# A decoder trunk on one core: five blocks of the stream turned by VectorE blocks and DMA instead of TensorE

## The chip, the cores and the metric

The kernel runs on 1 core of one Trainium2 chip. The time is the device time of one execution, in microseconds; lower is better. All times of before in this document come from one profiled execution or from the three timed runs beside it. "TensorE", "VectorE", "ScalarE", "GpSimd" and "SyncE" are the engines that the profile calls PE (its weight loads PEld), DVE, ACT, POOL and SP.

## What is computed

The reference is a two-layer decoder trunk on one sequence of 256 tokens with 2048 channels, in f32. Layer 0 mixes by causal pooling, layer 1 by latent attention with a shared key and value set; each layer ends in a SwiGLU FFN of width 5632. Cut to what matters:

```python
def modulate(h, shift, scale):
    return h * (1.0 + scale[:, None, :]) + shift[:, None, :]

h = modulate(rmsnorm(x, norm_mix[i]), shift_m, scale_m)
cq = rmsnorm(h @ w_dq, q_norm)              # queries, layer 1
q = (cq @ w_uq).reshape(B, S, H, Q_HEAD_DIM)
...
x = x + gate_m[:, None, :] * y
h = modulate(rmsnorm(x, norm_ffn[i]), shift_f, scale_f)
x = x + gate_f[:, None, :] * ((silu(h @ w_gate) * (h @ w_up)) @ w_down)
```

The shifts, scales and gates are themselves products of a 2048-vector with 2048 x 12288 weights per layer.

## The kernel before

The residual stream `x` lies in SBUF with tokens on the partitions: two token tiles of 128, each with 2048 channels, which the code treats as four blocks of 512 (`ND = 4`, `CH = 512`). A projection needs the stream the other way round, channels on the partitions. So each block is scaled by the norm (`scaled`, line 546, two pieces of 128 x 512), turned, and then modulated per channel (`modulated`, line 571).

Products are made to f32 accuracy from fp32r halves: every weight unit (512 x 512, 1 MB) is loaded by SyncE, ScalarE makes its upper half (`hl`, line 376), VectorE the rest as a lower half (line 378), and each block of the stream becomes an upper and a lower half in the same way (lines 583, 584). A unit is then 24 matmuls of 128 x 512 on line 422, in the order upper weight by upper block, upper weight by lower block, lower weight by upper block (`proj_unit`).

The turning has two forms. `turned_pieces` (line 558) uses TensorE: 8 transposes of 128 x 128 a block into PSUM (line 564). The FFN's inner activations of some chunks use the other form: VectorE turns 32 x 32 blocks in place (line 752), GpSimd's queue stores the tile to DRAM (line 754) and loads it back in another order (line 769); the weights that meet it have their rows permuted to fit.

Where the stream blocks are turned in layer 1:

- Queries: `hidden_q` makes the four blocks `hmx[0]` to `hmx[3]`. The first two are turned; the last two were kept, turned, from the shared keys and values. They are read by the four units of `w_dq`, which stand on TensorE behind the keys and values of the third group of heads (`keys_values(2)`, lines 1386 and 422) and ahead of those of the fourth. The query latent's norm (`Latent.norm`, lines 1336 to 1339) and its own 8 transposes (`Latent.turn`) follow.
- Last FFN: `start_ffn(1, ...)` begins six chunks at once. For each of its blocks it runs 12 units; block 0 has a path of its own (`first`), blocks 1 to 3 are scaled by `ahead(j + 1)` a few units before they are turned and modulated by `hidden(j + 1, pieces)`.

Beside all this runs a background: the modulation sums of later stages (line 213), one 1 MB weight tile each, a load on SyncE and one pass on VectorE; `plan` and `tick` say how many go with each unit.

A tile framework gives out buffers and semaphores and sets the order of each engine's instructions by its own estimates; the engines then run their lists in order. The buffers that matter here are the seven of the tag `t2k` (2 KB a partition: scaled pieces, turned tiles, reloaded tiles, whole modulated columns), six `raw` (loaded weights), six `hl` (halves of weights) and eight banks of PSUM (`ps`).

Of the kernel before, what the change touches and what calls it, by code (L numbers as in the profile page):

```python
# [17 lines left out]
P = 128  # L18
# [77 lines left out]
def tile_trunk(ctx: ExitStack, tc: tile.TileContext, a: dict, out: bass.AP):  # L96
# [22 lines left out]
    def t2k(shape, dt=F32):  # L119
        return work.tile(shape, dt, tag="t2k", bufs=7, name=nm("t2k"))  # L120
# [437 lines left out]
    def turned_pieces(pieces):  # L558
# [7 lines left out]
            pts.append(pt)  # L566
        return pts

    mod_ins, hid_ins = [None], [None]

    def modulated(pts, j, c_scale, c_shift, direct=False):
        flush()
# [165 lines left out]
    def ffn(l, hT, gate_name, begun, then):  # L738
# [7 lines left out]
            return proj(ffn_weights(l)[which][:, c], hT)  # L746

        def turn_blocks(c):
            turned[c] = []
            for tok in range(NT):  # L750
                blocks = t2k([P, CH])
                dve.transpose(out=blocks, in_=nat[c][tok])  # L752
                rows = dram.tile([P, CH], F32, name=nm("turned"))
                pool.dma_start(rows, blocks)  # L754
                turned[c].append(rows)

        def turned_halves(m, tok, full):
            order = "p k (b j) -> p k b j"
# [5 lines left out]
        def transposed(c):  # L764
            m = act_t([P, 2, KL, T])
            if c in TURNED_BY_DMA[l]:
                for tok in range(NT):
                    full = t2k([P, CH])
                    pool.dma_start(full.rearrange("p (b e) -> p b e", e=P),
                                   turned[c][tok].rearrange("(b i) (g e) -> (i g) b e", i=BLOCK, e=P))  # L770
                    halves = lambda tok=tok, full=full: turned_halves(m, tok, full)
                    if c == GROUPS[-1][0]:
                        halves()
                    else:
                        pending.append((1, halves))
                mids[c] = m
                return
            for tok in range(NT):
                pt = ps_t()
                for f in range(KL):  # L780
                    pe.transpose(pt[:, f * P:(f + 1) * P], nat[c][tok][:, f * P:(f + 1) * P], ident)  # L781
                v = pt.rearrange("p (f t) -> p f t", f=KL)
                ts_ = slice(tok * P, (tok + 1) * P)
                act.activation(m[:, 0, :, ts_], v, AF.Copy)
                dve.tensor_tensor(out=m[:, 1, :, ts_], in0=v, in1=m[:, 0, :, ts_].bitcast(F32), op=ALU.subtract)
            mids[c] = m
# [143 lines left out]
    def start_ffn(l, first, ahead, hidden, late):  # L930
# [3 lines left out]
        with tc.issue_after(mod_ins[0].ins), tc.issue_after(hid_ins[0].ins) if hid_ins[0] else nullcontext():  # L934
            for j in range(ND - 1):
                if l == 0 and j == 1:
                    for tok in range(NT):
                        sync.dma_start(aside[0][:, tok], back[tok])
                todo = KD // 2 if j + 1 >= ND - late else 0
                for n, (c, which) in enumerate((c, w) for c in begun for w in (GATE, UP)):  # L940
                    if n == 2 * len(begun) - 1:
                        hT.append(hidden(j + 1, pieces))
                    if l == 0 or j > 0 or c > 0:
                        begun[c][which].block(j, hT[j])
                    if n == 2 * len(begun) - 5:
                        pieces = ahead(j + 1)
                    if todo and (n > 1 or j > 0 or l > 0):
                        pump(1)
                        todo -= 1
                pump(todo)  # L950
# [440 lines left out]
    with tc.issue_after(mod_ins[0].ins):  # L1391
        kv = [keys_values(0)]
    hmx = []
    pieces = scaled(rstd, 0)

    def hidden_q():
        nonlocal pieces
        pts = turned_pieces(pieces) if len(hmx) < 2 else kept[len(hmx) - 2]
        if len(hmx) < 1:
            pieces = scaled(rstd, len(hmx) + 1)  # L1400
        hmx.append(modulated(pts, len(hmx), C_AM1, C_SM1))

    def last_of_background():
        plan(n_all + MIX_DQ, 0)
# [253 lines left out]
    def first(pair):  # L1658
# [14 lines left out]
        with tc.manual_schedule(engines=ordered):  # L1673
# [28 lines left out]
            run(g1[0], g1[1], u1[0], u1[1], g1[2], u1[2])  # L1702
        return h.hT[0]

    hT, begun = start_ffn(1, first, lambda j: scaled(rstd, j),
                          lambda j, pieces: modulated(turned_pieces(pieces), j, C_AF1, C_SF1), LATE)
    plan(0, FFN1_UNITS)
    ffn(1, hT, "ffn1", begun, lambda: None)

# [5 lines left out]
    return w.reshape(k // CH, n // CH, P, KL * CH)  # L1715


def laid_out(i):

    def columns(v):  # L1720
        return np.asarray(v).reshape(-1, P).T

    o = {n: np.asarray(i[n]) for n in ("x", "c", "positions", "mod_w", "final_norm")}
    o["vectors"] = np.concatenate([columns(i[n]) for n in (
        "c", "norm_mix", "norm_ffn", "kv_in_norm", "kv_norm", "q_norm", "pool_scale", "mod_b", "kv_mod_b")], 1)
    o["mod_wt"] = o["mod_w"].transpose(0, 2, 1)
    o["kv_mod_wt"] = np.asarray(i["kv_mod_w"]).T
    block = o["mod_w"][0].reshape(KD // 2, 2, P, 6, D)[:, :, :, 3:5, :CH]
    o["mod_block"] = block.transpose(0, 2, 1, 3, 4).reshape(KD // 2, P, 4 * CH)

# [6 lines left out]
    for n in ("w_dkv", "w_uk", "w_uv"):  # L1737
        o[n] = units(np.asarray(i[n]))
    o["pool_w"] = np.asarray(i["pool_w"])[0].reshape(-1, KL, P, CH).transpose(0, 2, 1, 3).reshape(-1, P, KL * CH)
    for n in ("w_dq", "w_o"):  # L1740
        o[n] = units(np.asarray(i[n])[0])
    for n in ("ffn_gate", "ffn_up", "ffn_down"):
        o[n] = np.stack([units(w) for w in np.asarray(i[n])])
    for l, chunks in enumerate(TURNED_BY_DMA):
        w = np.asarray(i["ffn_down"])[l].reshape(NF, KL, KL, BLOCK, ND, CH)[list(chunks)]
        o["ffn_down"][l, list(chunks)] = w.transpose(0, 4, 3, 1, 2, 5).reshape(len(chunks), ND, P, KL * CH)
    return o


# [16 lines left out]
```

## Time and profile before

| | us |
|---|---|
| median of 3 runs | 1890.53 (1888.92 to 1891.82) |
| profiled execution | 1889.67 |
| its span, first to last instruction | 1887.9 |
| TensorE busy | 1836.0 |
| VectorE busy | 1431.6 |
| ScalarE busy | 836.2 |
| GpSimd busy | 56.1 |

The granted TensorE clock is 0.992 on the mean. A group's line in the profile gives the source line, the engine, the operation, output<-input, count, busy time and mean length in ns. The chain of waits gives start, length, engine and line of what the end of the run hung on. "DMA to landing" is the time from the issue of a transfer until its last byte is there. The stages: conditioning sums and pooling to 166 us, first FFN to some 880 us, keys and values and queries from there to 997 us, heads to 1085, output projection to 1145, last FFN to the end.

### The profile page before, as it was taken

What the parts mean: (1) busy time and instruction counts of PE and PEld (TensorE: products, weight loads), DVE (VectorE), ACT (ScalarE), POOL (GpSimd) and SP (SyncE); (2) the same over time, 40 slices, a digit from 0 to 9 for tenths busy, and PEclk for the clock granted to TensorE, in tenths of its full rate; (3) what the DMA queues carried; (4) which work ended last, traced back from release to release, by engine and by line L of the source; (5) the groups of instructions that cost most, each with busy time, mean ns of one, the idle gap of its engine ahead of it and who ended that gap; (6) DMA issues with size and microseconds to landing.
All of it is one profiled execution on the core that took longest, in us unless ns stands there. A gap on an engine that the chain in (4) does not pass through costs nothing.

```text
span 1887.9 us, 21743 instructions
## 1 busy us (share of the span) xinstructions
PE 1836.0 (97%) x8629; PEld 1489.2 (79%) x8629; DVE 1431.6 (76%) x1437; ACT 836.2 (44%) x914; POOL 56.1 (3%) x82
## 2 busy tenths in 40 slices
PE   6689999999999999999999999999999999999998
PEld 2356888888888888888889888888888888888886
DVE  1247799999889798897898886889778666645557
ACT  3125643453433334344776635634444433443343
POOL 0000000000000000000110000000011000000000
PEclk9889999999999999999999999999999999999999
DMA  9999998889999899995594485988788776766651
GB/s 399 415 420 411 387 365 335 322 311 367 406 350 420 346 407 390 392 420 205 200 376 166 168 342 199 386 328 333 264 312 318 293 268 237 267 253 235 223 200 45
DMA packets 84280, 589.14 MB, mean 312 GB/s; under 512 B 9761, under 2 KB 10193, under 8 KB 15441
## 3 DMA queue, kind: packets, MB, share of 16 engines
q1 hardware_dynamic: 79346, 570.68, 77.8%
q0 software_dynamic: 4592, 16.78, 2.4%
q8 instruction: 68, 1.11, 0.2%
q10 hardware_dynamic: 240, 0.29, 0.0%
q14 instruction: 34, 0.28, 0.0%
HBM read 574.58 MB, written 13.13 MB: 311 GB/s over the span
## 4 chain that ended last, share of the span: by engine, by line
PE 93%; DMA 5%; DVE 0%; ACT 0%; SPq 0%; issue 0%; POOLq 0%; DVEq 0%; ACTq 0%
PE ps L422 80%; DMA raw<-in_mod_w_dram 5%; PE ps L431 2%; PE ps L1033 2%; PE ps L1386 1%; PE ps L258 1%; PE ps L1472 1%; PE ps L1578 1%; PE ps L1289 1%; PE ps L781 0%; PE ps L564 0%; PE ps L1475 0%; DMA raw<-in_mod_block_dram 0%; PE ps L1487 0%; PE ps L1527 0%; PE ps L1488 0%
## 5 line engine op out<-in xcount | busy, mean ns | idle before, releaser
L422 PE MATMUL ps<-hl,act 128*128 128x512 f32 x6672 | 1518.5, 389 | 0.0
L422 PEld LDWEIGHTS ps<-hl,act 128*128 128x128 f32 x6672 | 1250.3, 188 | 260.2 <-ACT act L1108 0.9
L376 ACT ACTIVATE hl<-raw 128x2048 fp32r<-128x2048 f32 x285 | 545.8, 1918 | 638.2 <-PE ps L422 413.0
L378 DVE TENSOR_TENSOR hl<-raw,hl 128x2048 fp32r<-128x2048 f32 x285 | 651.3, 2287 | 196.6 <-ACT hl L376 196.5
L213 DVE SCALAR_TENSOR_TENSOR raw<-raw,s_row 128x2048 f32<-128x2048 f32 x168 | 383.1, 2284 | 15.5 <-DMA raw<-in_mod_wt_dram 15.4
L258 PE MATMUL ps<-raw,s_strip 128*32 128x512 f32 x392 | 59.0, 688 | 38.3 <-DMA raw<-in_mod_w_dram 37.9
L722 DVE TENSOR_TENSOR act<-ps,act 128x512 f32<-128x512 f32 x96 | 63.9, 682 | 15.4 <-PE ps L422 15.4
L258 PEld LDWEIGHTS ps<-raw,s_strip 128*32 128x32 f32 x392 | 8.8, 116 | 68.7 <-DMA raw<-in_mod_w_dram 47.6
L431 PE MATMUL ps<-hl,act 128*128 128x512 f32 x192 | 47.6, 400 | 0.6 <-DVE act L527 0.5
L431 PEld LDWEIGHTS ps<-hl,act 128*128 128x128 f32 x192 | 35.1, 188 | 10.3 <-ACT act L514 2.5
L794 DVE TENSOR_TENSOR x<-ps,x 128x512 f32<-128x512 f32 x32 | 21.6, 688 | 20.0 <-PE ps L422 20.0
L544 DVE TENSOR_TENSOR hl<-raw,hl 128x2048 fp32r<-128x2048 f32 (+3 forms) x17 | 31.9, 1879 | 4.8 <-ACT hl L541 4.7
L265 DVE COPY t2k<-ps 128x256 f32<-128x256 f32 x4 | 1.7, 425 | 44.3 <-ACT t2k L264 44.3
L1033 PEld LDWEIGHTS ps<-act,act 128*128 128x128 f32 x128 | 25.0, 202 | 11.7 <-issue 8.4
L754 POOL DMA_DIRECT2D turned<-t2k x26 | 14.5, 556 | 649.6 <-DVE t2k L752 649.3
L451 ACT ACTIVATE junk<-x 128x512 bf16<-128x512 f32 x23 | 14.5, 629 | 42.1 <-DVE x L636 25.0
L856 ACT ACTIVATE t2k<-ps 128x512 f32<-128x512 f32 x24 | 14.2, 592 | 41.8 <-PE ps L422 41.8
L1033 PE MATMUL ps<-act,act 128*128 128x256 f32 x128 | 32.4, 406 | 0.0
L720 ACT ACTIVATE act<-ps 128x512 f32<-128x512 f32 x32 | 19.1, 596 | 29.2 <-PE ps L422 29.2
L860 DVE TENSOR_TENSOR t2k<-ps,t2k 128x512 f32<-128x512 f32 x24 | 16.5, 687 | 19.9 <-PE ps L422 19.9
L541 ACT ACTIVATE hl<-raw 128x2048 fp32r<-128x2048 f32 (+1 forms) x15 | 26.5, 1766 | 3.5 <-PE ps L422 3.5
L998 DVE COPY hl<-ps 128x256 f32<-128x256 f32 x4 | 1.7, 423 | 30.4 <-PE ps L997 30.4
(235 smaller groups left out, 1044.3 us busy)
## 6 DMA issues: line engine op xcount, KB each, us to landing
raw<-in_mod_wt_dram SPq DMA_DIRECT2D x136, 1024.0 KB, 6.8
raw<-in_ffn_up_dram SPq DMA_DIRECT2D x88, 1024.0 KB, 6.5
raw<-in_ffn_down_dram SPq DMA_DIRECT2D x88, 1024.0 KB, 6.8
raw<-in_ffn_gate_dram SPq DMA_DIRECT2D x87, 1024.0 KB, 6.5
raw<-in_mod_w_dram SPq DMA_DIRECT2D x48, 1024.0 KB, 13.8
raw<-in_kv_mod_wt_dram SPq DMA_DIRECT2D x32, 1024.0 KB, 9.6
raw<-in_w_o_dram SPq DMA_DIRECT2D x16, 1024.0 KB, 5.4
raw<-in_mod_block_dram SPq DMA_DIRECT2D x8, 1024.0 KB, 12.5
```

The lines of the kernel that those rows point to most:

```text
L213: dve.scalar_tensor_tensor(out=r, in0=r, scalar=1.0, in1=s_row, op0=ALU.mult, op1=ALU.mult, accum_out=self.sums[:, self.n:self.n + 1])
L258: pe.matmul(self.bank[m * STRIP:(m + 1) * STRIP, :], lhsT=weights(k), rhs=r[:, k, i, :], start=first, stop=last)
L376: hi_ins = act.activation(hi, r, AF.Copy)
L378: lo_ins = dve.tensor_tensor(out=lo, in0=r, in1=hi.bitcast(F32), op=ALU.subtract)
L422: pe.matmul(banks[tok], lhsT=t_[:, i, k, tok * P:(tok + 1) * P], rhs=w[:, k, :], start=first and n < len(part), stop=last and n >= len(ord ...
L431: pe.matmul(bank, lhsT=t_[:, i, k, tok * P:(tok + 1) * P], rhs=w[:, k, :], start=first and n == 0, stop=last and n == len(order) - 1)
L541: hid_ins[0] = act.activation(w[1], w[0], AF.Copy)
L544: dve.tensor_tensor(out=w[2][:, ks], in0=w[0][:, ks], in1=w[1][:, ks].bitcast(F32), op=ALU.subtract)
L720: act.activation(part, banks[tok], AF.Copy)
L722: dve.tensor_tensor(out=part, in0=banks[tok], in1=part, op=ALU.add)
L794: dve.tensor_tensor(out=sums, in0=bank, in1=sums, op=ALU.add)
L1033: pe.matmul(mixed[g][:, n % 2, :], lhsT=wp[g][:, k, ns], rhs=pool_all[g // 2][:, g % 2, k, :], start=k == 0, stop=k == KL - 1)
```

## The change

Five blocks, `hmx[0]` and `hmx[1]` of the queries and blocks 1 to 3 of the last FFN, take the second form of turning. `stored_blocks` turns both scaled pieces on VectorE and stores them; `loaded_blocks` loads a block back in two halves of 256 channels (`pairs`), two transfers each; `modulated_blocks` modulates from these tiles instead of PSUM. The weights and vectors that meet these blocks (`w_dq`, `ffn_gate` and `ffn_up` of layer 1, the norms, the layer's modulation) have their rows permuted ahead of time, which costs the chip nothing. The two query blocks are scaled, turned and stored before the second group of keys and values is written; the reload of the second is written behind the modulation of the first. In the last FFN `ahead` comes four units earlier. The scratch for the descriptors of GpSimd's transfers (`dynamic_dma_scratch_size`) goes from 1024 to 4096.

```diff
+    def stored_blocks(pieces):
+        stored = []
+        for piece in pieces:
+            blocks = t2k([P, CH])
+            dve.transpose(out=blocks, in_=piece)
+            rows = dram.tile([P, CH], F32, name=nm("turned"))
+            pool.dma_start(rows, blocks)
+            stored.append(rows)
+        return stored
+
+    def channels_first(rows):
+        return rows.rearrange("(b i) (g e) -> (i g) b e", i=BLOCK, e=P)
+
+    def turned_by_dma(pieces):
+        return loaded_blocks(stored_blocks(pieces))
+
+    def loaded_blocks(stored):
+        pairs = [t2k([P, NT * KL, 2 * BLOCK]) for _ in range(2)]
+        for tok in range(NT):
+            for h2 in range(2):
+                es = slice(2 * h2 * BLOCK, 2 * (h2 + 1) * BLOCK)
+                pool.dma_start(pairs[h2][:, tok * KL:(tok + 1) * KL, :], channels_first(stored[tok])[:, :, es])
+        return pairs
...
+    def modulated_blocks(pairs, j, c_scale, c_shift):
+        flush()
+        t_ = act_t([P, 2, KL, T])
+        for k in range(KL):
+            scale, bias = (cols[:, i, j * KL + k:j * KL + k + 1] for i in (c_scale, c_shift))
+            full, src = t2k([P, T]), pairs[k // 2][:, :, k % 2 * BLOCK:(k % 2 + 1) * BLOCK]
+            act.activation(full.rearrange("p (b j) -> p b j", j=BLOCK), src, AF.Identity, scale=scale, bias=bias)
+            act.activation(t_[:, 0, k, :], full, AF.Copy)
+            mod_ins[0] = dve.tensor_tensor(out=t_[:, 1, k, :], in0=full, in1=t_[:, 0, k, :].bitcast(F32), op=ALU.subtract)
+        return t_
...
-                    if n == 2 * len(begun) - 5:
+                    if n == 2 * len(begun) - (9 if l == DEPTH - 1 else 5):
                         pieces = ahead(j + 1)
...
-    pieces = scaled(rstd, 0)
+    stored = [stored_blocks(scaled(rstd, j)) for j in range(2)]
+    pairs = loaded_blocks(stored[0])
 
     def hidden_q():
-        nonlocal pieces
-        pts = turned_pieces(pieces) if len(hmx) < 2 else kept[len(hmx) - 2]
-        if len(hmx) < 1:
-            pieces = scaled(rstd, len(hmx) + 1)
-        hmx.append(modulated(pts, len(hmx), C_AM1, C_SM1))
+        nonlocal pairs
+        j = len(hmx)
+        hmx.append(modulated_blocks(pairs, j, C_AM1, C_SM1) if j < 2 else modulated(kept[j - 2], j, C_AM1, C_SM1))
+        if j == 0:
+            pairs = loaded_blocks(stored[1])
...
-    hT, begun = start_ffn(1, first, lambda j: scaled(rstd, j),
-                          lambda j, pieces: modulated(turned_pieces(pieces), j, C_AF1, C_SF1), LATE)
+    hT, begun = start_ffn(1, first, lambda j: turned_by_dma(scaled(rstd, j)),
+                          lambda j, pairs: modulated_blocks(pairs, j, C_AF1, C_SF1), LATE)
...
-    nc = bacc.Bacc("TRN2", target_bir_lowering=False, num_devices=1, dynamic_dma_scratch_size=1024)
+    nc = bacc.Bacc("TRN2", target_bir_lowering=False, num_devices=1, dynamic_dma_scratch_size=4096)
```

In the changed kernel the old lines 376, 378, 213 keep their numbers; 1387 (copy of keys) is 1415, 1378 (copy of values) is 1406, 582 and 583 are 601 and 602 for the five blocks and 617 and 618 for the kept ones, 1337 and 1339 are 1365 and 1367, 912 is 940.

TensorE's list loses the 40 transposes (4566 rows become 4526) and is otherwise the same, but for two matmuls that change place around the query latent's transposes. SyncE's list is the same.

GpSimd's queue in the queries' stage was empty; now these twelve transfers stand there between the two norms (`t2k_6346` and `t2k_6347` are the two halves of block 0, `t2k_6533` and `t2k_6534` those of block 1; `turned_6328` and `turned_6332` are the stores of block 0, `turned_6340` and `turned_6344` those of block 1):

```order
L575 DMA turned_6328<-t2k_6326 128x512
L575 DMA turned_6332<-t2k_6330 128x512
L590 DMA t2k_6346<-turned_6328 128x4x64
L575 DMA turned_6340<-t2k_6338 128x512
L575 DMA turned_6344<-t2k_6342 128x512
L590 DMA t2k_6347<-turned_6328 128x4x64
L590 DMA t2k_6346<-turned_6332 128x4x64
L590 DMA t2k_6347<-turned_6332 128x4x64
L590 DMA t2k_6533<-turned_6340 128x4x64
L590 DMA t2k_6534<-turned_6340 128x4x64
L590 DMA t2k_6533<-turned_6344 128x4x64
L590 DMA t2k_6534<-turned_6344 128x4x64
```

What moved: nothing, these are new. The buffers of the built program tie them further: `t2k_6347` lies where store 2 reads from, so its first load waits for that store to land; `t2k_6533` and `t2k_6534` lie where `t2k_6346` and `t2k_6347` lay, so block 1's loads wait until ScalarE has scaled from block 0's.

ScalarE in the queries' stage, before: from the weight split of the first unit of `w_dq` (`raw_6606`) over block 0 (`act_6504`) to the split of the third (`raw_6689`). The copies on lines 1387 and 1378 are keys and values of the third group.

```order
L376 ACTIVATE hl_6611<-raw_6606 128x2048
L1378 ACTIVATE act_6326<-ps_6389 128x512
L1387 ACTIVATE act_6425<-ps_6438 128x512
L376 ACTIVATE hl_6661<-raw_6656 128x2048
L582 ACTIVATE t2k_6505<-ps_6490,cols 128x256
L582 ACTIVATE t2k_6509<-ps_6490,cols 128x256
...
L583 ACTIVATE act_6504<-t2k_6517 128x256
L1387 ACTIVATE act_6425<-ps_6464 128x512
L1378 ACTIVATE act_6425<-ps_6521 128x512
L376 ACTIVATE hl_6694<-raw_6689 128x2048
```

The same place now (`act_6516` is block 0, `act_6573` block 1; `raw_6664` and `raw_6697` are the second and third unit of `w_dq`):

```order
L376 ACTIVATE hl_6619<-raw_6614 128x2048
L1406 ACTIVATE act_6352<-ps_6415 128x512
L601 ACTIVATE t2k_6517<-t2k_6346,cols 128x256
...
L602 ACTIVATE act_6516<-t2k_6529 128x256
L376 ACTIVATE hl_6669<-raw_6664 128x2048
L1415 ACTIVATE act_6451<-ps_6490 128x512
L1406 ACTIVATE act_6451<-ps_6539 128x512
L601 ACTIVATE t2k_6574<-t2k_6533,cols 128x256
...
L1406 ACTIVATE act_6451<-ps_6540 128x512
L376 ACTIVATE hl_6702<-raw_6697 128x2048
L602 ACTIVATE act_6573<-t2k_6582 128x256
```

What moved: block 0's rows now stand ahead of the second unit's split and the first copy of keys (`ps_6464`), and a copy and the third unit's split stand inside block 1, ahead of its last two upper halves.

VectorE around the query latent's norm, before (613 and on) and after:

```order
L378 TENSOR_TENSOR hl_6866<-raw_6856,hl_6865 128x2048
L1337 TENSOR_SCALAR sm_6757<-sm_6756 128x1
L213 SCALAR_TENSOR_TENSOR raw_6858,sums_5369<-raw_6858,s_row 128x2048
L1339 TENSOR_SCALAR t2k_6759<-ps_6587,sm_6758 128x512
L1337 TENSOR_SCALAR sm_6766<-sm_6765 128x1
L213 SCALAR_TENSOR_TENSOR raw_6861,sums_5369<-raw_6861,s_row 128x2048
L1339 TENSOR_SCALAR t2k_6768<-ps_6588,sm_6767 128x512
```

Now:

```order
L1365 TENSOR_SCALAR sm_6765<-sm_6764 128x1
L213 SCALAR_TENSOR_TENSOR raw_6784,sums_5369<-raw_6784,s_row 128x2048
L378 TENSOR_TENSOR hl_6874<-raw_6864,hl_6873 128x2048
L1367 TENSOR_SCALAR t2k_6767<-ps_6595,sm_6766 128x512
L1365 TENSOR_SCALAR sm_6774<-sm_6773 128x1
L213 SCALAR_TENSOR_TENSOR raw_6866,sums_5369<-raw_6866,s_row 128x2048
L1367 TENSOR_SCALAR t2k_6776<-ps_6596,sm_6775 128x512
```

What moved: the weight's lower half (line 378) went from ahead of the norm into it. Further up on VectorE, the two lower halves of block 1's last two pieces stand behind the `krT` row (line 940), a background sum and the third unit's lower half.

More of the change, by code (lines that the diff above doesn't have):

```diff
@@ L748, in turn_blocks @@
         def turn_blocks(c):
[L749 to L755, printed above, removed]
+            turned[c] = stored_blocks(nat[c])
         def turned_halves(m, tok, full):
@@ L768, in transposed @@
                     full = t2k([P, CH])
-                    pool.dma_start(full.rearrange("p (b e) -> p b e", e=P),
-                                   turned[c][tok].rearrange("(b i) (g e) -> (i g) b e", i=BLOCK, e=P))
+                    pool.dma_start(full.rearrange("p (b e) -> p b e", e=P), channels_first(turned[c][tok]))
                     halves = lambda tok=tok, full=full: turned_halves(m, tok, full)
@@ L1715, in units, with by_blocks @@
     return w.reshape(k // CH, n // CH, P, KL * CH)
+def by_blocks(v, blocks):
+    o, n = np.array(v), [CH * b + r for b in blocks for r in range(CH)]
+    w = o[n].reshape((len(blocks), KL, KL, BLOCK) + o.shape[1:])
+    o[n] = w.transpose((0, 2, 3, 1) + tuple(range(4, w.ndim))).reshape((-1,) + o.shape[1:])
+    return o
 def laid_out(i):
@@ L1721, in columns @@
         return np.asarray(v).reshape(-1, P).T
-    o = {n: np.asarray(i[n]) for n in ("x", "c", "positions", "mod_w", "final_norm")}
+    i = {n: np.asarray(v) for n, v in i.items()}
+    o = {n: i[n] for n in ("x", "c", "positions", "mod_w", "final_norm")}
+    early, late = range(2), range(1, ND)
+    turned = [g * ND + j for gs, js in (((0, 1), early), ((3, 4), late)) for g in gs for j in js]
+    last = [by_blocks(m, turned) for m in (i["mod_w"][1].T, i["mod_b"][1])]
+    i["norm_mix"] = np.stack([i["norm_mix"][0], by_blocks(i["norm_mix"][1], early)])
+    i["mod_b"] = np.stack([i["mod_b"][0], last[1]])
+    i["norm_ffn"] = np.stack([i["norm_ffn"][0], by_blocks(i["norm_ffn"][1], late)])
     o["vectors"] = np.concatenate([columns(i[n]) for n in (
         "c", "norm_mix", "norm_ffn", "kv_in_norm", "kv_norm", "q_norm", "pool_scale", "mod_b", "kv_mod_b")], 1)
-    o["mod_wt"] = o["mod_w"].transpose(0, 2, 1)
-    o["kv_mod_wt"] = np.asarray(i["kv_mod_w"]).T
+    o["mod_wt"] = np.stack([i["mod_w"][0].T, last[0]])
+    o["kv_mod_wt"] = i["kv_mod_w"].T
     block = o["mod_w"][0].reshape(KD // 2, 2, P, 6, D)[:, :, :, 3:5, :CH]
@@ L1739, in laid_out @@
     o["pool_w"] = np.asarray(i["pool_w"])[0].reshape(-1, KL, P, CH).transpose(0, 2, 1, 3).reshape(-1, P, KL * CH)
[L1740 to L1746, printed above, removed]
+    o["w_dq"] = units(by_blocks(i["w_dq"][0], early))
+    o["w_o"] = units(i["w_o"][0])
+    for n in ("ffn_gate", "ffn_up"):
+        o[n] = np.stack([units(i[n][0]), units(by_blocks(i[n][1], late))])
+    o["ffn_down"] = np.stack([units(by_blocks(w, chunks)) for w, chunks in zip(i["ffn_down"], TURNED_BY_DMA)])
     return o
```

## Prediction

> **What bounds the kernel now.** I read the page first, then the chain of waits, then the busy times in the two stages that the change touches. The page says that TensorE carries nearly the whole span:
>
> ```profile
> span 1887.9 us, 21743 instructions
> PE 1836.0 (97%) x8629; PEld 1489.2 (79%) x8629; DVE 1431.6 (76%) x1437; ACT 836.2 (44%) x914; POOL 56.1 (3%) x82
> PE 93%; DMA 5%; DVE 0%; ACT 0%; SPq 0%; issue 0%; POOLq 0%; DVEq 0%; ACTq 0%
> ```
>
> The 5% of DMA lies in the first 160 us. After that, a microsecond of TensorE work that disappears is a microsecond of the span, and so is every microsecond for which TensorE has to wait for something new. The chain of waits, at the places where the blocks are turned (start, duration):
>
> ```profile
> 955.75 0.87 PE ps L564 x8
> 956.62 5.49 PE ps L422 x24
> 962.12 0.87 PE ps L564 x8
> 962.99 21.78 PE ps L422 x96
> 984.76 5.75 PE ps L1386 x48
> 991.43 0.66 PE ps L564 x6
> 992.09 4.80 PE ps L422 x21
> ...
> 1217.10 0.87 PE ps L564 x8
> 1217.97 65.30 PE ps L422 x288
> 1283.28 0.87 PE ps L564 x8
> ...
> 1349.45 0.87 PE ps L564 x8
> ```
>
> The first two groups of eight are the queries' blocks, the last three the FFN's. No gap stands around any of them. The 96 products from 962.99 are the four query blocks, 24 each at 0.227 us: 5.45 us a block.
>
> The other views that matter are the DMA share of some stretches, and how long the existing turned stores and reloads take to land. In the table, the last three columns are the granted clock, the DMA share and GB/s:
>
> ```profile
> 935.00:975.00 40.00, 40.00 (x231) 35.30 (x230) 39.93 (x41) 32.00 (x53) 0.00 (x0) 1.00 1.00 402
> 546.00:568.00 22.00, 22.00 (x99) 18.22 (x98) 21.96 (x18) 5.76 (x3) 2.65 (x4) 1.00 0.99 387
> 699.00:721.00 22.00, 22.00 (x99) 18.22 (x98) 20.84 (x16) 7.25 (x6) 2.65 (x4) 1.00 1.01 397
> 1638.00:1741.00 103.00, 103.00 (x456) 85.16 (x456) 55.36 (x38) 40.60 (x28) 8.48 (x13) 1.00 0.69 254
> ```
>
> In the queries' stage, 935 to 975, TensorE, VectorE (39.93 of 40) and DMA (1.00) are all full. In just such full stretches (546 to 721), the six turned stores and the six reloads landed after:
>
> ```profile
> L754 POOL DMA_DIRECT2D turned<-t2k x6: 542/558/569, 546.6 to 699.6; - x6
> DMA to landing us min/median/max: 5.4/6.8/8.0
> L769 POOL DMA_DIRECT2D t2k<-turned x6: 759/770/775, 552.6 to 713.5; - x6
> DMA to landing us min/median/max: 6.8/7.2/7.7
> ```
>
> Over the whole run the stores take 2.3/5.2/10.0 and the reloads 3.1/6.9/10.5 (least, median, most):
>
> ```profile
> DMA to landing us min/median/max: 2.3/5.2/10.0
> DMA to landing us min/median/max: 3.1/6.9/10.5
> ```
>
> **The change part by part.** *TensorE loses* 5 groups of 8 transposes: 5 x 0.87 = 4.35 us, all on the chain. That is 0.23% of the profiled execution's 1889.67 us, hardly more than the 0.2% that a measurement of this kernel can tell from no change.
>
> *The FFN's three blocks.* Each adds two VectorE transposes (row below), two stores and four reloads. Their scaled pieces exist at 1166.02, and the first block's columns are wanted after one more group of 24 products behind 1217.10, at 1222.5. With some 13 us of VectorE rows ahead of the transposes, 6.8 for a store, 3 for the issues and 7.2 for a reload, everything is there by about 1197. The cover is 25 us, and more than 40 for the other two blocks, so I cost this at nothing; gone, it would cost what it is late.
>
> ```profile
> L752 DVE STREAM_TRANSPOSE t2k<-t2k x26: 668/704/712, 545.6 to 1726.6; 128x512 f32<-128x512 f32 x26
> 1166.02 1.36 ACT L554 ACTIVATE t2k<-x,rstd 128x512 f32<-128x512 f32 x2
> ```
>
> *The queries' two blocks.* Here the cover is thin. These are the rows of before from which I walk the new order (the order itself is in the fences above):
>
> ```profile
> 937.11 2.29 DVE L378 TENSOR_TENSOR hl<-raw,hl 128x2048 fp32r<-128x2048 f32 x1
> 950.95 0.57 ACT L1378 ACTIVATE act<-ps 128x512 f32<-128x512 f32 x1
> 954.77 1.70 DVE L912 TENSOR_TENSOR krT<-t2k 32x256 f32<-32x256 f32 x4
> 957.12 1.00 ACT L582 ACTIVATE t2k<-ps,cols 128x256 f32<-128x256 f32 x2
> 958.02 0.72 ACT L583 ACTIVATE act<-t2k 128x256 fp32r<-128x256 f32 x2
> 960.15 0.60 ACT L1387 ACTIVATE act<-ps 128x512 f32<-128x512 f32 x1
> 961.24 1.92 ACT L376 ACTIVATE hl<-raw 128x2048 fp32r<-128x2048 f32 x1
> ```
>
> Let a store land S after its issue, a reload L after its issue. The first transpose follows the 937.11 row (its pitch is 2.2 us): store 1 is issued at 940.0. One L378 and one transpose later, at 942.9, comes store 2. Block 0's last three reloads wait for store 2 to land, because the second half's buffer is the one that store 2 reads, and are issued 0.77 apart. ScalarE's first row on block 0 needs the third of the four: 943.7 + S + L. With 6.8 and 7.2 that is 957.7. ScalarE has stood since 951.5, with a copy of keys and a weight split behind it; those have several us in hand. From there three scalings (0.5 each), a copy (0.5) and the first upper half (0.36) make 960.2. TensorE wants it at 962.99 - 1.74 = 961.25, so block 0 is just in time: nothing.
>
> Block 1 is not. Its reloads write the buffers of block 0, so the first waits for block 0's second scaling, the second for the fourth, at 957.7 + 3.6 = 961.3. The third of them, issued at 962.1, lands at 962.1 + 7.2 = 969.3. In general this is 948.1 + S + 2L. TensorE wants block 1's first upper half at 961.25 + 5.45 = 966.7, so ScalarE has to begin 1.36 earlier, at 965.3: it is 4.0 late. Then ScalarE's order puts a copy (0.6) and a weight split (1.9) between the third and fourth scaling and their upper halves: the third upper half comes 5.6 after ScalarE's begin, where TensorE wants it 1.36 + 0.91 after: 3.3 more. VectorE's order puts the krT row (1.70), a background sum (2.2) and a weight's lower half (2.2) ahead of the last two lower halves: 1.2 more. Sum 8.5. Bounds: with the fast ends (2.3 and 3.1) S + 2L is 8.5 and no term is left; with the slow ends (10.0 and 10.5) it is 31.0, the lateness 13.8 and the sum 18.3. I take the middle, since the rows of the full stretches are nearest: same queue, same DMA share.
>
> *The query norm behind it.* After the change VectorE does a weight's lower half (2.29) more between the first norm's small row (L1337) and the row that scales by it (L1339); the transposes of the query latent wait for these.
>
> ```profile
> 983.95 0.15 DVE L1337 TENSOR_SCALAR sm<-sm 128x1 f32<-128x1 f32 x1
> 984.01 2.29 DVE L213 SCALAR_TENSOR_TENSOR raw<-raw,s_row 128x2048 f32<-128x2048 f32 x1
> 986.74 0.75 DVE L1339 TENSOR_SCALAR t2k<-ps,sm 128x512 f32<-128x512 f32 x1 [0.43 <-POOL sm L1338]
> 990.19 0.75 DVE L1339 TENSOR_SCALAR t2k<-ps,sm 128x512 f32<-128x512 f32 x1 [0.43 <-POOL sm L1338]
> ```
>
> Before, the second L1339 ends at 990.94 and the last six transposes begin at 991.43. The extra row, less the 0.43 that VectorE waited anyway, is 1.9 us. Bounds: 0, if VectorE has caught up while TensorE stands, and 4.5, two rows.
>
> *The four times larger scratch.* Before, the second of two reloads is issued only when the first has landed:
>
> ```profile
> 706.11 0.76 POOL L769 DMA_DIRECT2D t2k<-turned  x1 [5.98 <-DMA turned<-t2k]
> 713.54 0.77 POOL L769 DMA_DIRECT2D t2k<-turned  x1 [6.67 <-issue]
> ```
>
> So the old scratch held one reload of 128 x 4 runs and not two; four times that holds the four reloads of a block, which have as many runs each, half as long. This I have used above. For the old FFN chunks it brings their reloads about 7 us forward. TensorE waits for none of them now, so this is worth nothing; below nothing neither, because nothing is queued behind them on GpSimd's queue but their like. SyncE's order of loads does not change. The added 2 MB in the queries' stage are 5 us at its 402 GB/s; they push the weights back, which had 6 to 10 us in hand. That is in the upper bound only.
>
> Sum: -4.35 + 8.5 + 1.9 = +6.05 on 1889.67, that is 1895.7 us. The median of the runs shown, 1890.53, stands 0.86 higher; I forecast on the profiled execution.
>
> **The rivals.** *A, the reloads are quick.* TensorE keeps its full 4.35: 1885.3 us, or 1887.2 if the norm's 1.9 stays. It decides at S + 2L below 12.7 (17.2, less 3.3 and 1.2). Stores landing after 2.3 and reloads after 3.1 speak for it, but those least values lie outside the full stretches; the full stretches themselves, at 19 and more, speak against it. [...]
>
> *B, the reloads land in time, but the order costs.* With S + 2L at 17.2 the lateness is gone, and 3.3 + 1.2 + 1.9 - 4.35 = +2.05 remain: 1891.7 us, no change that can be told. For it: ScalarE and VectorE stand for a while, so they free fewer weight buffers, SyncE issues fewer loads, and block 1's reloads may meet an emptier DMA than block 0's. Against it: VectorE goes on with four rows meanwhile.
>
> *C, the slow ends.* Reloads of 256-byte runs, with eight transfers queued behind each other, land as late as the latest rows: 18.3 + 1.9 - 4.35 = +15.9, 1905.5 us.
>
> **How the numbers follow.** The forecast gets 0.50, its own range 1893.5 to 1901. A gets 0.22, B 0.20, C 0.08. Faster by over 0.2% is A, 0.22; within it is B, 0.20; slower is the forecast and C, 0.58. The range goes down to 1885 to hold A, and up to 1903, leaving out most of C.
>
> **What would show it.** In the changed kernel the L564 rows fall from 72 to 32. Right would be: TensorE gaps behind the first 24 products of the queries' first block, in sum near 8 us and released by ScalarE (the upper halves) and VectorE (the lower halves); ScalarE's wait for the reload near 6 us from 951; no gap at 1217, 1283 and 1349. Wrong would be: the 96 products in one piece (A), or gaps of 4 to 5 us with the reloads of block 1 landing within 5 us (B), or TensorE waiting for weights in the FFN.

## The result, and the profile after

| | before | after |
|---|---|---|
| median of the runs beside each other | 1890.34 us (1888.92 to 1891.82) | 1901.58 us (1900.67 to 1902.55) |
| profiled span | 1887.9 | 1900.0 |
| granted TensorE clock, mean | 0.992 | 0.986 |
| L564 transposes on TensorE | 72 | 32 |

The changed kernel is slower: ratio 1.006, 95% interval 1.005 to 1.007. The forecast was 1895.7 us; the time lies in its range and on the side it gave the most chance, 5.9 us above the number and 0.6 us above the forecast's own range, 1893.5 to 1901. The loss of 11.2 us is nearly twice the 6.05 of the sum. The mean clock of one execution says little here: the fast runs of before span 0.986 to 0.993. In the page of the changed kernel, the span, the busy times and the chain by engine:

```profile
span 1900.0 us, 21734 instructions
PE 1839.8 (97%) x8589; PEld 1489.3 (78%) x8589; DVE 1437.5 (76%) x1447; ACT 837.3 (44%) x914; POOL 76.3 (4%) x112
PE 90%; DMA 6%; DVE 2%; issue 1%; ACT 1%; POOL 0%; SPq 0%; POOLq 0%; DVEq 0%; ACTq 0%
```

TensorE has 40 instructions fewer and is nevertheless 3.8 us longer busy (1836.0 before): the same products took longer somewhere. TensorE is 90% of the chain, 93% before. Its waits in the queries' stage and ahead of the heads, by what ended them (us in total, times, longest):

```profile
...
PE ps L422 <- ACT act L602: 7.1, 3, 5.0
...
PE ps L294 <- DVE cols L302: 2.0, 1, 2.0
```

Where they stand, in TensorE's timeline of the changed kernel (start, duration, count, idle time before and its releaser):

```profile
961.72 5.95 PE L422 MATMUL ps<-hl,act 128*128 128x512 f32 x24 [0.27 <-ACT act L602]
972.69 2.07 PE L422 MATMUL ps<-hl,act 128*128 128x512 f32 x4 [5.03 <-ACT act L602]
976.57 18.57 PE L422 MATMUL ps<-hl,act 128*128 128x512 f32 x68 [1.80 <-ACT act L602]
994.98 5.92 PE L1414 MATMUL ps<-act,hl 128*128 128x256 f32 x48
...
1002.63 0.88 PE L564 MATMUL ps<-con,t2k 128*128 128x128 f32 x6 [0.36 <-DVE t2k L1367]
...
1009.92 0.34 PE L294 MATMUL ps<-con,cols 128*16 128x128 f32 x1 [2.04 <-DVE cols L302]
```

Line 302 on VectorE ends the sums of a gate; TensorE turns their columns (`cols`) on line 294 before it goes on to the heads. The same products before, and what follows them:

```profile
962.75 22.02 PE L422 MATMUL ps<-hl,act 128*128 128x512 f32 x96
984.60 5.92 PE L1386 MATMUL ps<-act,hl 128*128 128x256 f32 x48
```

The 96 products of the queries' blocks now run from 961.72 to 994.98, 33.26 us from start to start against 21.85. Only 6.83 us of the difference are the waits of 5.03 and 1.80; the other 4.58 are in the products. Four of them took 2.07 us (972.69), 0.52 each against 0.227. The granted clock says why (busy times with counts, then clock, DMA share and GB/s):

```profile
967.50:972.60 5.10, 0.16 (x1) 0.00 (x0) 0.00 (x0) 1.36 (x4) 0.00 (x0) 0.99 0.93 312
972.60:976.50 3.90, 2.07 (x4) 1.16 (x4) 3.76 (x7) 3.90 (x8) 0.00 (x0) 0.50 0.04 15
976.50:980.00 3.50, 3.43 (x8) 2.51 (x9) 3.50 (x5) 3.50 (x11) 0.00 (x0) 0.50 0.47 112
982.00:985.00 3.00, 3.00 (x13) 2.40 (x12) 3.00 (x3) 3.00 (x8) 0.00 (x0) 0.89 0.75 309
1009.90:1012.60 2.70, 2.68 (x13) 2.70 (x14) 1.54 (x1) 0.27 (x1) 0.00 (x0) 0.52 0.78 246
```

After the wait of 5.03 us TensorE works at half clock (0.50) for about 10 us, and after the wait of 2.04 us ahead of the heads once more (0.52) for about 3.4. In the kernel before, the clock is 1.00 in both places.

The transfers behind the waits, on GpSimd's queue and on ScalarE:

```profile
940.59 0.63 POOL L575 DMA_DIRECT2D turned<-t2k  x1 [17.91 <-DVE t2k L573]
950.15 2.25 POOL L590 DMA_DIRECT2D t2k<-turned  x3 [0.46 <-issue]
960.56 0.75 POOL L590 DMA_DIRECT2D t2k<-turned  x1 [8.16 <-ACT t2k L601]
963.08 2.23 POOL L590 DMA_DIRECT2D t2k<-turned  x3 [1.77 <-ACT t2k L601]
```

```profile
959.00 1.09 ACT L601 ACTIVATE t2k<-t2k,cols 128x256 f32<-128x256 f32 x2 [6.22 <-DMA t2k<-turned]
971.24 1.09 ACT L601 ACTIVATE t2k<-t2k,cols 128x256 f32<-128x256 f32 x2 [5.25 <-DMA t2k<-turned]
974.31 1.90 ACT L376 ACTIVATE hl<-raw 128x2048 fp32r<-128x2048 f32 x1
```

Block 1's reloads are issued when ScalarE has scaled from block 0's (960.56, 963.08) and land for 971.24; the weight split that ScalarE does inside block 1 (974.31) stands ahead of the upper half that ends the second wait.

In the last FFN nothing waits. From the first full group of products on, TensorE's work is one piece to the end of the window shown (1400), where before it was cut by transposes at 1217, 1283 and 1349:

```profile
1182.65 217.54 PE L422 MATMUL ps<-hl,act 128*128 128x512 f32 x959
```

Against before, the trace runs 10.4 us late at the fourth group's keys (994.98), 11.4 at the query latent's last six transposes (1002.63), 14.7 at the end of the heads, and 12.1 at the end of the span: the FFN gives 2.6 us back.

### The profile page after: what moved, and what is told of

Same layout as the page of the kernel before. It is cut to its first block, busy times and chain, and to the rows that moved or that the text cites. A ratio compares the mean times of both kernels' runs of the same rounds, so it can differ in the third digit from the quotient of the medians.

```text
span 1900.0 us, 21734 instructions
## 1 busy us (share of the span) xinstructions
PE 1839.8 (97%) x8589; PEld 1489.3 (78%) x8589; DVE 1437.5 (76%) x1447; ACT 837.3 (44%) x914; POOL 76.3 (4%) x112
## 4 chain that ended last, share of the span: by engine, by line
PE 90%; DMA 6%; DVE 2%; issue 1%; ACT 1%; POOL 0%; SPq 0%; POOLq 0%; DVEq 0%; ACTq 0%
PE ps L422 77%; DMA raw<-in_mod_w_dram 4%; PE ps L431 2%; PE ps L1061 2%; PE ps L258 2%; DMA t2k<-turned 1%; PE ps L1501 1%; PE ps L1607 1%; DVE raw L213 1%; PE ps L1317 1%; DVE hl L378 0%; DMA raw<-in_ffn_gate_dram 0%; PE ps L809 0%; PE ps L1504 0%; DMA raw<-in_mod_block_dram 0%
## 5 line engine op out<-in xcount | busy, mean ns | idle before, releaser
L575 POOL DMA_DIRECT2D turned<-t2k x36 | 20.1, 558 | 661.5 <-DVE t2k L573 661.2
L573 DVE STREAM_TRANSPOSE t2k<-t2k 128x512 f32<-128x512 f32 x36 | 24.8, 701 | 3.5 <-DMA turned<-t2k 3.2
```

The source lines that it names most:

```text
L573: dve.transpose(out=blocks, in_=piece)
```

## Experiments

Ratios are to the kernel before, run beside each kernel on the same chip, with their 95% intervals. The intervals are some 2 us wide on each side, so terms of a microsecond are read from the traces.

**1 to 3: the parts one by one.** First the FFN's three blocks alone, with the queries' two back on TensorE:

```diff
-    early, late = range(2), range(1, ND)
+    early, late = (), range(1, ND)
...
-    stored = [stored_blocks(scaled(rstd, j)) for j in range(2)]
-    pairs = loaded_blocks(stored[0])
+    pieces = scaled(rstd, 0)
```

> Only the last FFN's three blocks are turned by VectorE and DMA; the queries' two are back on TensorE; the scratch is 4096. Theory (the whole loss lies in the queries' stage, the FFN's transfers are covered): 24 transposes of 0.109 us go and nothing waits, -2.6 us, about 1887.9 us against 1890.5, ratio 0.9986; TensorE's products of the last FFN in one piece from the first reload on. Rival (turning by DMA costs in itself, by its traffic or GpSimd's queue, about the same in every block): three fifths of the +11.2 us, 1897 us, ratio 1.0035, with gaps in the last FFN.

Measured: 1887.51 against 1890.7 us, ratio 0.9982 (0.9972 to 0.9991). Its last FFN is unbroken like that of the changed kernel. The theory holds: the three blocks bring what their transposes cost.

Then the queries' two alone:

```diff
-    early, late = range(2), range(1, ND)
+    early, late = range(2), ()
...
-                    if n == 2 * len(begun) - (9 if l == DEPTH - 1 else 5):
+                    if n == 2 * len(begun) - 5:
...
-    hT, begun = start_ffn(1, first, lambda j: turned_by_dma(scaled(rstd, j)),
-                          lambda j, pairs: modulated_blocks(pairs, j, C_AF1, C_SF1), LATE)
+    hT, begun = start_ffn(1, first, lambda j: scaled(rstd, j),
+                          lambda j, pieces: modulated(turned_pieces(pieces), j, C_AF1, C_SF1), LATE)
```

> Only the queries' two blocks are turned by VectorE and DMA; the last FFN's three are back on TensorE; the scratch is 4096. Theory (the loss lies in the queries' stage): the changed kernel's +11.2 without the FFN's -2.6, that is +13.8 us, about 1904.3 us, ratio 1.0073, with the same two gaps of 5 and 2 us on TensorE and a granted clock near 0.5 behind each. Rival (a like cost in every block): two fifths of +11.2, 1895 us, ratio 1.0024.

Measured: 1903.55 us, ratio 1.0068 (1.0055 to 1.008). TensorE's waits behind the first block are those of the changed kernel, 4.62 and 1.80 among the products and 2.04 ahead of the heads. But here the first block is late as well, by 1.95 us, where the changed kernel has 0.27:

```profile
963.75 5.92 PE L422 MATMUL ps<-hl,act 128*128 128x512 f32 x24 [1.95 <-ACT act L602]
974.29 2.08 PE L422 MATMUL ps<-hl,act 128*128 128x512 f32 x4 [4.62 <-ACT act L602]
```

The loss lies in the queries' stage, whole.

Then the scratch alone (`dynamic_dma_scratch_size=4096` in the kernel before):

> The kernel before with nothing changed but the scratch for descriptors, 4096 instead of 1024. Theory: the two reloads of an FFN chunk are now issued together, the second some 7 us earlier, and nobody waits for them: 0, ratio within 0.999 to 1.001. Rival (the earlier reloads are what shortens the last FFN, not the missing transposes): -2.6 us, ratio 0.9986; or, if they crowd out weights, above 1.002.

Measured: 1889.48 us, ratio 0.9992 (0.9983 to 1.0001), no difference that can be told from none. It does what was said of it: the second reload of a chunk is now issued 1.77 us after the first, where it was 7.43 (706.11 and 713.54 before). GpSimd's queue in this run:

```profile
705.95 0.76 POOL L769 DMA_DIRECT2D t2k<-turned  x1 [6.37 <-DMA turned<-t2k]
707.72 0.77 POOL L769 DMA_DIRECT2D t2k<-turned  x1 [1.01 <-DMA turned<-t2k]
```

**4: own buffers for the reloads.** If block 1 is late because its reloads wait for block 0's buffers, buffers of their own take that away:

```diff
...
-    pairs = loaded_blocks(stored[0])
+    both = act_t([P, 4, NT * KL, 2 * BLOCK], F32)
+    own.extend([both[:, 2 * j], both[:, 2 * j + 1]] for j in range(2))
+    pairs, pairs1 = (loaded_blocks(s) for s in stored)
```

> The changed kernel, but the reloads of the queries' two blocks go to a buffer of 8 KB of their own (a slot of the blocks' tag), so block 1's no longer wait for block 0 to be scaled; TensorE's and SyncE's lists are as in the changed kernel. Theory (the lateness is the chain of reload, scaling, reload through shared buffers): block 1's reloads are issued near 956 instead of 960.6 to 963.8 and are there near 966; the gap of 5.0 us behind the first 24 products falls below 1.5, the granted clock behind it stays over 0.9, and the 96 products take 24 to 26 us instead of 33.3: about 1893.5 us (1892 to 1897). The wait of 2 us ahead of the heads stays. Rival (the DMA is full, so eight reloads together land as late as two times four): the gap stays at 4 us or more and the time at 1900 or above.

Measured: 1901.37 us, ratio 1.0052 (1.0038 to 1.0066). The theory falls. The wait behind the first 24 products has gone, but block 0 now comes late. TensorE, ScalarE and GpSimd of this run:

```profile
967.08 20.52 PE L422 MATMUL ps<-hl,act 128*128 128x512 f32 x78 [6.74 <-ACT act L603]
```

```profile
961.89 1.09 ACT L602 ACTIVATE t2k<-act,cols 128x256 f32<-128x256 f32 x2 [13.11 <-DMA act<-turned]
962.89 1.89 ACT L376 ACTIVATE hl<-raw 128x2048 fp32r<-128x2048 f32 x1
```

```profile
957.72 1.49 POOL L590 DMA_DIRECT2D act<-turned  x2 [6.00 <-DMA turned<-t2k]
```

Block 0 was there 2.9 us later than in the changed kernel (961.89 against 959.00), although its last three reloads were issued earlier (949.47 against 950.15); why they took longer is not shown. A weight split of 1.9 us got between its scaling and its upper halves. Block 1's reloads still wait, for its stores: issued from 948.40 on, these land at 957.7, after 9 us. So in these two builds the buffers decide which block is late, not whether one is.

**5: no pause for TensorE.** Twenty products that nobody reads fill the wait:

```diff
         proj_unit(cq, hmx[j], hi, lo, j == 0, j == ND - 1)
+        if j == 0:
+            spare = ps_t()
+            for n in range(20):
+                k = n % KL
+                pe.matmul(spare, lhsT=hmx[0][:, 0, k, :P], rhs=hi[:, k, :], start=n == 0, stop=n == 19)
```

> The changed kernel with 20 spare products of 128x512 (into a bank that nobody reads) on TensorE between the first 24 products of the queries and the next, 4.5 us in the place of the 5.0 us wait; they are extra work, and the output is unchanged. In this build ScalarE's copy and weight split also move out of block 1, and the gate's cols row (L302) comes ahead of the head weights on VectorE. Theory (the wait halves the granted clock, and that costs 4.6 us in the products and 1.3 at the heads on top of the waits): the granted clock stays at 1.00 through the stage, the last 72 products take 16.4 us instead of 22.3 (waits counted), and the time is about 1892 us (1890 to 1895). Rival (the low clock in the records costs nothing, the products are late for their halves of weights): only the moved rows help, 1.8 and 2.0 us, 1897.5 us or more, with gaps among the 72 products.

Measured: 1904.28 us, ratio 1.0076 (1.0062 to 1.009). The theory is right on the clock and nearly right on the products (18.7 us, 16.4 expected), and wrong on the time. The clock stays at 1.00, and the last 72 products, from 972.33, end at 991 instead of 995. But more than these 4 us is lost again at the norm behind them (the windows of this run, then VectorE, then TensorE):

```profile
972.30:991.00 18.70, 17.32 (x72) 13.45 (x73) 18.62 (x25) 16.67 (x28) 0.00 (x0) 1.00 0.63 234
1001.60:1011.00 9.40, 6.44 (x20) 5.22 (x21) 7.91 (x10) 5.53 (x9) 2.46 (x1) 0.52 0.87 282
```

```profile
972.30 0.76 DVE L603 TENSOR_TENSOR act<-t2k,act 128x256 fp32r<-128x256 f32 x2 [5.32 <-ACT act L602]
```

```profile
1001.65 0.45 PE L564 MATMUL ps<-con,t2k 128*128 128x128 f32 x1 [4.66 <-DVE sm L1365]
1005.00 1.76 PE L564 MATMUL ps<-con,t2k 128*128 128x128 f32 x7 [2.91 <-DVE t2k L1367]
```

VectorE stood for 5.32 us while block 1 was late, and from then on has hardly a gap until the norm (18.62 busy of 18.70). TensorE waits there for VectorE, 4.66 and 2.91 us, and the clock halves there instead. VectorE is as full as TensorE in this stage (39.93 of 40 us before), so its own pause is work that TensorE waits for later. What this run does not settle is the price of the clock in the end time.

**6 to 8: more cover, and the row ahead of the heads.** The four blocks are a sum, so the kept ones can go first:

```diff
-    hmx = []
+    hmx, ORDER = [], (2, 3, 0, 1)
...
-        j = len(hmx)
+        j = ORDER[len(hmx)]
...
-        hi, lo = w_unit(a["w_dq"][j, 0])
+        hi, lo = w_unit(a["w_dq"][ORDER[j], 0])
```

> The changed kernel with the queries' four blocks summed in the order 2, 3, 0, 1, the kept ones first, so that the two turned blocks are wanted 10.9 us later; same work. Theory (both blocks are late for want of cover, whatever the cause of the slow reloads): block 0 is there by 962 and block 1 by 973, against 972 and 977.6 wanted; the 96 products stand in one piece of 21.8 us, the clock at 1.00. The extra row in the norm (1.0) and the wait for the gate's cols row (2.0, and up to 1.3 of slow clock) stay, so -4.35 + 3.0 to 4.3: 1889 to 1890.5 us, ratio 0.9995. Rival (more cover only shifts the reloads, since block 1's wait for ScalarE, which now scales block 0 behind two kept blocks): a gap of 3 us or more ahead of the last 24 products, 1894 us or more.

Measured: 1894.25 us, ratio 1.0021 (1.001 to 1.0031). Cover takes most of the loss away, but not to the expected 1889 to 1890.5. The time is the rival's, its mechanism is not: among the products only one wait of 1.23 us is left, not 3; at the norm there are two, and the heads' is as it was:

```profile
979.67 5.36 PE L422 MATMUL ps<-hl,act 128*128 128x512 f32 x22 [1.23 <-ACT act L602]
...
992.33 0.41 PE L564 MATMUL ps<-con,t2k 128*128 128x128 f32 x2 [1.54 <-DVE sm L1365]
...
995.68 0.87 PE L564 MATMUL ps<-con,t2k 128*128 128x128 f32 x6 [1.79 <-DVE t2k L1367]
...
1002.97 0.27 PE L294 MATMUL ps<-con,cols 128*16 128x128 f32 x1 [2.06 <-DVE cols L302]
```

The row ahead of the heads was moved by itself, in the changed kernel:

```diff
-            dve.tensor_tensor(out=col, in0=sums, in1=bias(first, KD), op=ALU.add)
+            with tc.high_priority(offset=2000):
+                dve.tensor_tensor(out=col, in0=sums, in1=bias(first, KD), op=ALU.add)
```

> The changed kernel with one row moved: the gate's cols row (L302) gets a high priority and stands three rows earlier on VectorE, behind the first split of the head weights. Theory (TensorE's 2.0 us ahead of the heads and the slow clock behind it come from that row alone): both go, -3.3 us against the changed kernel, 1898.3 us. Rival (VectorE's lower halves of the query latent, which stand around it, are as late and take its place as the releaser): a wait of 1.5 us or more stays ahead of the heads, 1900.5 us or more.

Measured: 1896.79 us, ratio 1.0035 (1.0022 to 1.0048), some 4.8 us below the changed kernel. The wait ahead of L294 is gone, and the clock there is 1.00. The theory holds. Of the 5.0 us between the two profiled spans (1895.0 and 1900.0), 2.2 are there already at the fourth group's keys (992.78 against 994.98), since the clock comes back some 3 us sooner after the long wait of this run (0.50 from 973 to 977 and 0.70 to 981, against 0.50 to 981 and 0.79 to 985); that is not the row's doing. At the norm it loses 1.0 of them again (1001.38 against 1002.63); the 3.7 us from there to the end are the row's, where 3.3 were expected. Where the row stands on VectorE, in the kernel before and in the changed kernel:

```profile
990.86 0.17 DVE L302 TENSOR_TENSOR cols<-sums,vcol 128x16 f32<-128x16 f32 x1
```

```profile
1009.61 0.17 DVE L302 TENSOR_TENSOR cols<-sums,vcol 128x16 f32<-128x16 f32 x1
```

Both edits together:

> Both edits, the kept blocks first and the gate's cols row early. Theory: all that is left of the loss is the extra row in the norm (1.0): -4.35 + 1.0, about 1887 us, ratio 0.998, faster than the kernel before and level with the version that turns only the FFN's blocks by DMA. Rival (the lower halves take the cols row's place ahead of the heads): 1888.5 to 1890.5 us, no better than the order of the blocks alone.

Measured: 1891.18 us, ratio 1.0004 (0.9996 to 1.0013): level with before, where 1887 was expected. The wait ahead of the heads is gone, so it is not the rival's row that holds TensorE either. What is left is a wait of 0.71 us among the products and two at the norm:

```profile
991.39 0.41 PE L565 MATMUL ps<-con,t2k 128*128 128x128 f32 x2 [1.54 <-DVE sm L1366]
...
994.75 0.88 PE L565 MATMUL ps<-con,t2k 128*128 128x128 f32 x6 [1.80 <-DVE t2k L1368]
```

That is 4.05 us in all, about the 4.35 of the transposes. Against the version that turns only the FFN's blocks, the queries' two cost about 4 us even with cover, by the two ratios (1.0004 and 0.9982).

**9: VectorE's rows alone.** The kernel before with the scratch at 4096, the four transposes on VectorE added and nothing else:

```diff
...
+    def also(pieces):
+        for piece in pieces:
+            dve.transpose(out=t2k([P, CH]), in_=piece)
```

> The kernel before, scratch 4096, with four VectorE transposes of 128x512 added in the queries' stage, of the two blocks' scaled pieces, their results unread; the blocks are still turned by TensorE and nothing is stored. Theory (VectorE is as full there as TensorE, so rows added on VectorE come back as a wait of TensorE at the query latent's norm): four rows of 0.65 us, 2.6 us, some 1893 us (1892 to 1895), ratio 1.0014, with waits of TensorE behind L1337 and L1339 that the kernel before does not have. Rival (VectorE has room, what cost was the lateness of the reloads alone): 1890.5 us, ratio 1.000.

Measured: 1892.15 us, ratio 1.0008 (1.0000 to 1.0017). It stands on the edge of what can be told; the trace shows the mechanism, a wait at the norm that the kernel before does not have:

```profile
994.07 0.87 PE L564 MATMUL ps<-con,t2k 128*128 128x128 f32 x6 [1.51 <-DVE t2k L1343]
```

So the two blocks' turning costs VectorE about as much on the path (1.5) as it saves TensorE (1.74).

**10 and 11: the transfers alone.** The kernel before, with the four stores and eight reloads added, of pieces that are not turned; the reloaded tiles are not read.

> The kernel before, scratch 4096, with the queries' four stores and eight reloads added on GpSimd's queue (the scaled pieces as they are, the reloaded tiles unread); TensorE, VectorE and SyncE have the same lists as before. Theory (the weights have 6 to 10 us in hand): 2 MB more in the stage cost nothing that shows, ratio 0.9995 to 1.0005. Rival (with the DMA full, 2 MB at 402 GB/s are 5 us that nothing makes up): up to +5 us, 1893 us or more, with waits for weights or for VectorE rows on weights.

Measured: 1898.72 us, ratio 1.0047 (1.0033 to 1.0061). But this run has a fault as a test of traffic: the reloaded tiles take places among the seven `t2k` buffers, and ScalarE's scaling of block 0, which writes to such buffers, had to wait for one until a reload had landed in it. ScalarE, TensorE and the window behind:

```profile
967.22 0.56 ACT L593 ACTIVATE t2k<-ps,cols 128x256 f32<-128x256 f32 x1 [6.34 <-DMA t2k<-turned]
```

```profile
969.25 24.92 PE L422 MATMUL ps<-hl,act 128*128 128x512 f32 x96 [5.12 <-ACT act L594]
```

```profile
969.20:975.00 5.80, 5.75 (x16) 4.53 (x17) 4.91 (x7) 5.80 (x11) 0.00 (x0) 0.59 0.98 390
```

What it shows well is the price of one wait. TensorE's list is that of before and it waits for little else: behind 5.12 us of waiting the same 96 products took 2.90 us longer (24.92 against 22.02 in the same view of before), with the clock at 0.59. Of the 8.2 us of this run these two are 8.0.

The reloads were then given a buffer of their own, which leaves the lists of all engines but GpSimd as before:

```diff
-        pairs = [t2k([P, NT * KL, 2 * BLOCK]) for _ in range(2)]
+        if not own:
+            both = act_t([P, 4, NT * KL, 2 * BLOCK], F32)
+            own.extend([both[:, 2 * j], both[:, 2 * j + 1]] for j in range(2))
...
```

> The kernel before, scratch 4096, with the queries' four stores and eight reloads added as in the run of the transfers alone, but the reloaded tiles lie in a buffer of their own, so that no row of ScalarE has to wait for a reload to land; the lists of TensorE, VectorE, ScalarE and SyncE are the same as before. Theory (the run of the transfers alone lost its 8.2 us by the wait of ScalarE for a buffer that a reload still held, 5.1 us, and the halved clock behind it, 3.1): both go, 1890.5 to 1892 us, ratio 0.9995 to 1.001, the granted clock at 1.00. Rival (the 2 MB themselves push the weights back): 1893 us or more, with TensorE waiting for halves of weights.

Measured: 1895.44 us, ratio 1.0035 (1.0023 to 1.0048). The rival holds: 2 MB of traffic in this stage cost by themselves. The profiled execution, 1893.56 us, is the fastest of its six, so its trace shows some 4 us of the 5.5. ScalarE's split of the second weight unit of `w_dq`, in the kernel before and in this run:

```profile
955.30 1.92 ACT L376 ACTIVATE hl<-raw 128x2048 fp32r<-128x2048 f32 x1 [1.80 <-PE ps L1386]
```

```profile
959.80 1.92 ACT L376 ACTIVATE hl<-raw 128x2048 fp32r<-128x2048 f32 x1 [4.63 <-DMA raw<-in_w_dq_dram]
```

Before, ScalarE waits for TensorE there and the weight lies ready; now it waits 4.63 us for the weight, and block 0's scaling stands behind it. So the weight was there for 959.80; before, it was issued at 946.05 and landed 8.1 us later, and no weight of this stretch took over 9.0. TensorE waits in six small pieces of 0.2 to 0.7 us, 2.45 us in all, and the clock stays at 1.00.

**12: less work for VectorE.** The version with both edits (8), with twelve VectorE rows given to GpSimd:

> The kernel with the kept blocks first and the gate's cols row early, and twelve VectorE rows of the queries' stage (the four krT rows, 1.7 us, and the eight lower halves of the kept blocks, 2.8 us) given to GpSimd, which stands idle there. Theory (what is left of the loss is VectorE's want of time in the stage): the 1.5 and 1.8 us for which TensorE waits at the norm go, 1887 to 1888 us, ratio 0.9985. Rival (those waits are the order of rows and the way over GpSimd's power, not VectorE's load): they stay, 1890 us or more. A third: GpSimd is too slow with the lower halves, and TensorE waits among the kept blocks' products instead.

Measured: 1894.91 us, ratio 1.0027 (1.0018 to 1.0037), worse than without. Neither theory is tested, since GpSimd was too slow in another place than the third case said. Its queue:

```profile
933.86 11.06 POOL L941 TENSOR_TENSOR krT<-t2k 32x256 f32<-32x256 f32 x4 [12.65 <-DVE t2k L936]
944.87 1.17 POOL L576 DMA_DIRECT2D turned<-t2k  x2
```

The four krT rows take 2.7 us each there (0.42 on VectorE) and stand ahead of the stores, which go out at 944.87 instead of about 940; ScalarE then waits for the buffers that the stores read (6.47 us the longest). Of GpSimd's eight lower halves of 128x256 five took 3.51 us together and three 3.46 in the same run, so it is not the size that makes the krT rows (32x256) slow; what does is not shown.

The fastest version run is that of experiment 1. Whether more relief for VectorE would make the queries' blocks pay stays open.

## Why the prediction was right, and where its sum was off

The direction and the place are as forecast: the FFN's blocks bring their transposes (2.6 us, as in the sum), the scratch is worth nothing, block 0 is just in time (0.27 us), and the queries' second block is late by its reload. That block 0 came so near was in part luck: it was 0.8 us late in experiment 7 and 1.95 in experiment 2, with the same order of transfers. Block 0's scaling was put at 957.7 and came at 959.00; block 1's at 969.3 and came at 971.24, so S + 2L, taken as 21.2, was 2 us too short.

The terms that were mis-sized, in us:

| term | in the sum | measured |
|---|---|---|
| block 1: waits of TensorE | 8.5 | 5.03 + 1.80 |
| block 1: slow products behind them | none | 4.58 |
| query latent's norm | 1.9 | 1.0 |
| gate's cols row ahead of the heads | none | 2.04 |
| slow products behind it | none | about 1.5 |

- The waits for block 1 were sized 8.5 and were 6.8. The lateness was more than the 4.0 given (5.03), ScalarE's order cost 1.80 and not 3.3, and VectorE's 1.2 did not show. TensorE was at half clock by then: the four products ahead of the second wait took 2.07 us instead of 0.91, so a part of the price went from the wait into the products. That 6.8 lies near 8.5 comes in part from errors that offset each other.
- No step allowed for TensorE's clock after a wait. This is the largest miss, 6.1 us in two places.
- The wait for the cols row was not seen at all. The row's new place on VectorE, behind two splits of the head weights, is where it comes from (experiment 7).
- The step "they push the weights back, which had 6 to 10 us in hand" was wrong. The transfers alone cost 5.5 us by the medians (experiment 11). The second unit of `w_dq`, issued at 946.05 before and split at 955.30, had 1.2 us in hand, since it landed after 8.1 us (landings in that stretch took 5.5 to 9.0). In the changed kernel the price cannot be told apart from the lateness, so it is not added to the table.
- VectorE's four rows got no price, although the prediction quoted the row that says VectorE is full there. Alone they cost about 1.6 us by the medians, at the norm (experiment 9).

Rival A, by which the reloads would be quick, needed S + 2L below 12.7; it is refuted by 959.00 and 971.24. Rival B, the price of the order without the lateness, was put at +2.05; its nearest case, the kept blocks first, came out at some +4, with the wait for the cols row in it; without that wait (experiment 8) it was +1.2, and most of its waits stood at the norm.

That the FFN's transfers and transposes are covered and the queries' are not goes with the room in the stage. The kernel before, in the two stretches of the last FFN that now hold the added work (VectorE is the third engine's entry; the last two columns are the DMA share and GB/s):

```profile
1160.00:1240.00 80.00, 80.00 (x359) 65.97 (x358) 63.73 (x51) 48.56 (x56) 0.00 (x0) 1.00 0.88 345
1240.00:1350.00 110.00, 110.00 (x494) 91.21 (x494) 95.97 (x90) 42.99 (x31) 0.00 (x0) 1.00 0.83 310
```

There VectorE is 80 to 87% busy and the DMA share 0.83 to 0.88; in the queries' stage both stood at 1.00. But the FFN's blocks also had 25 us of cover and more by the prediction, and cover alone took most of the queries' loss away. No run separates the two for the FFN.

## What to carry to other kernels

A wait on the bounding engine has to be charged with what follows it: here 5.1 us of waiting cost 8.0. Before work is moved off the full engine, look at the room of the engines and queues that take it over, and at the cover, in that same stage: the same edit brought 3 us in the last FFN and cost 13 in the queries' stage, where VectorE (39.93 of 40 us) and DMA (share 1.00) were both full and the cover was thin. Where operands are summed, putting first the ones that need no transfer is a cheap cover (it took 7 of 11 us away).

## What the runs showed of the hardware

In these runs TensorE's granted clock fell to about half when TensorE had paused for long, and did not come back at once: 0.50 for about 10 us after waits of 5.03 and 1.80 us, 0.54 over 6 us after 6.74 (own buffers), 0.59 over 5.8 us after 5.12 (transfers alone). It fell after short pauses too, but not always: to 0.52 for about 3.4 us after 2.04 us in the changed kernel, and likewise after 2.04 us in the queries-only run (0.64 from 1012 to 1016), but it stayed at 1.00 after 2.06 and 2.08 us at the same place in the kept-first and own-buffers runs. Six pauses of under 0.8 us left it at 1.00 (experiment 11). Why a pause of some 2.05 us halved the clock in two runs and not in the others is not settled by these runs.

The transfers of 128 and 256 KB on GpSimd's queue landed late where the DMA was full (share 1.01 from 955 to 967.5 in the changed kernel): in the queries' stage the median was 7.2 us for a reload and 6.2 for a store in the changed kernel, 8.3 and 9.1 in the own-buffers run, where the least store of the kernel before took 2.3.
